# Expert outputs weighted and split at PSUM eviction, and combined by two fp32r passes with an exact one-hot matrix

## The chip, the cores and the metric

The kernel runs on one core of a Trainium2 chip, as one launch. The metric is device microseconds of one execution; the time of a kernel is the median of its runs. The engines are called by their short names below: PE (TensorE, matmuls), DVE (VectorE), ACT (ScalarE), POOL (GpSimd) and SP (SyncE, which issues the DMAs).

## What is computed

One layer of a hybrid encoder on 256 tokens of width 1024, in fp32: a mixer (attention beside a recurrence), a normalisation, and a mixture of 32 experts of which each token takes four. The change lies in the mixture, of which this is the core:

```python
logits = xt @ w_router + b_router
top_v, top_e = lax.top_k(logits, TOP_K)          # TOP_K = 4 of 32 experts
gates = jax.nn.softmax(top_v, axis=-1)
...
def expert_block(args):
    tok, g, e = args                             # the tokens of one expert
    xb = xt[tok]
    h = xb @ w_gu[e] + b_gu[e]
    y = clamped_swiglu(h) @ w_down[e] + b_down[e]
    return y * g[:, None].astype(y.dtype)        # weighted by the gate
...
out = jax.ops.segment_sum(ys.reshape(R, D), row_tok, num_segments=T)
x = layer_norm(ALPHA * x + moe(x), ln2_g, ln2_b)
```

## The kernel before

The experts' weights, 12 MB each, are streamed from HBM in transfers of 1 MB, eight of gate/up rows and four of down rows per expert, into 21 buffers that are filled in a fixed order (`load_chunk`, issued by SP). SP's and PE's instructions stand in the order of the code; those of DVE, ACT and POOL are ordered by a scheduler when the program is built. Every engine then works through its list in that order.

Each expert has 64 slots for tokens (`CAP`), and the 128 columns of PE hold two groups of 64. The loop over experts `e` does, on PE:

- `overflow(e)`: a branch on the number of the expert's tokens. Only with over 64 of them a slower spill-over pass (`more`) runs for the rest.
- `first(e)`: the gate/up matmuls `gu_mm` (L876, 64 records in the profile) into two PSUM tiles `h`, one for each half `b` of the expert's width. `swiglu` (L886 to L890) then turns each half into `g` on DVE and ACT: a minimum (L886), a sigmoid on ACT (L887), a clamp (L888), a product (L889), and the last product with the sigmoid (L890).
- `finish(e % 2)`: the combine of the pair of experts that ended before. The outputs of two experts lie in one tile of 128 partitions (64 slots each). `gt` holds, for every slot, a row over the 256 tokens with the gate at the slot's token and zero elsewhere; a matmul of `gt` with the outputs `y` (L938) adds each slot to its token, and DVE adds the result to `acc` (L940). One block of 128 tokens is done per expert: two matmuls, for the two halves of the 1024 columns.
- in an even expert `gate_rows` builds rows of gates per token for two experts on POOL; in an odd one `gate_t` transposes them into `gt` (L932, four transposes into one PSUM tile, and ACT's copy, L934).
- `act_t` for each half: two transposes of `g` (L897) and ACT's copy; `begin_gu` starts the next expert's `h` with the bias, an fp32r matmul (L668).
- `need`: the gather of the next pair's tokens (L786), and then the down matmuls `down_mm` (L909, 32 records) into the two PSUM tiles `ps[n]`.
- in an odd expert ACT copies `ps[n]` to `y` (L1105).

The PSUM tiles of `mc` (combine results, gate transposes, activation transposes, gather) share three banks. Combine and gate transposes before the change are fp32 matmuls; one fp32 matmul shows as two records of the profile, one fp32r matmul as one. Expert 31 ends differently: its weights' order, the pair before's last combines (`fin`, L1118) between the down matmuls of expert 30, and at the end ACT's and DVE's copies of `ps` (L1154, L1155), four `fin` matmuls and the last normalisation.

Of the kernel before, what the change touches and what calls it, by code (L numbers as in the profile page):

```python
# [9 lines left out]
F32 = mybir.dt.float32  # L10
F32R = mybir.dt.float32r
I32 = mybir.dt.int32
AF = mybir.ActivationFunctionType
OP = mybir.AluOpType
AX = mybir.AxisListType
ENG = mybir.EngineType

P = 128
D = 1024
T = 256  # L20
# [29 lines left out]
def trunk(ctx, tc, x, ln0_g, ln0_b, w_in, conv_w, conv_b, w_rg_a, b_rg_a, w_rg_x, b_rg_x,  # L50
# [4 lines left out]
    V, A, PE, G, SP = nc.vector, nc.scalar, nc.tensor, nc.gpsimd, nc.sync  # L55
# [14 lines left out]
    def f32(ap):  # L70
        return ap.bitcast(F32)

    def ps1(name):
        return psp.tile([P, 512], F32, tag="ps", name=name)

    def ps2(name):
        return pss.tile([P, 2, 512], F32, tag="sc", name=name)
# [129 lines left out]
    ident = keep.tile([P, P], F32, name="ident")  # L207
# [178 lines left out]
    def pj(c):  # L386
        return [psp.tile([P, 2, T], F32, tag="ps", name=f"pj{c}_{h}") for h in range(2)]
# [6 lines left out]
    ps = pj(0)  # L394
# [4 lines left out]
    ps = pj(1)  # L399
# [20 lines left out]
    ps = ps2("ps_lam")[:, 0]  # L420
# [52 lines left out]
    for b in range(4):  # L473
        V.tensor_scalar(xc[:, b], xl[:, b, 3:3 + T], pc[:, 3, b:b + 1], pc[:, 4, b:b + 1], op0=OP.mult, op1=OP.add)
        for w in range(3):
            V.scalar_tensor_tensor(xc[:, b], xl[:, b, w:w + T], pc[:, w, b:b + 1], xc[:, b],
                                   op0=OP.mult, op1=OP.add)
# [53 lines left out]
    for which, dst, bi in ((0, r_t, 5), (1, i_t, 6)):  # L531
        for h in range(2):
            ps = psp.tile([P, 2, T], F32, tag="ps", name=f"gate{which}_{h}")
            for m in range(2):
                PE.matmul(ps[:, m], wg[:, which, 2 * h + m], xc[:, 2 * h + m], start=True, stop=True)
            for m in range(2):
                b = 2 * h + m
# [29 lines left out]
    ps = ps1("gb1_ps")  # L567
# [6 lines left out]
    op = [ps2(f"op{qt}")[:, 0].rearrange("p (h c) -> p h c", h=H) for qt in range(NT)]  # L574
    for qt in range(NT):
        for h in range(H):
            for kt in range(qt + 1):
                PE.matmul(op[qt][:, h], sm[h][:, 1, (qt + kt) * P:(qt + kt + 1) * P], v_sb[:, kt, h * P:(h + 1) * P],
                          start=kt == 0, stop=kt == qt, skip_group_check=True)
# [53 lines left out]
    ps = ps2("cw_ps")[:, 0]  # L633
# [208 lines left out]
    wk = loop.enter_context(tc.tile_pool(name="wk", bufs=2, side="right", reuse_waits="tile"))  # L842
# [15 lines left out]
    def mc(name):  # L858
        return pmc[-1].tile([P, 512], F32, tag="gu", name=name)
# [52 lines left out]
    def dtiles(e):  # L912
        return [pdn.tile([P, 512], F32, tag=f"dn{n}", name=f"y{e}_{n}") for n in range(2)]

    def ytile(e, n):
        return wk.tile([P, 512], F32, tag=f"y{n}", bufs=1, name=f"ysb{e}_{n}")

    def gate_rows(e):

# [8 lines left out]
    def gate_t(e, sg):  # L928
        ps = mc(f"gt_ps{e}").rearrange("p (n t) -> p n t", n=2)
        for n in range(2):  # L930
            for t in range(NT):
                PE.transpose(ps[:, n, t * P:(t + 1) * P], sg[:, t, n * CAP:n * CAP + P], ident)  # L932
        gt = wk.tile([P, 2, T], F32, tag="gtT", bufs=1, name=f"gtT{e}")
        A.activation(gt, ps, AF.Copy)  # L934
        return gt

    def combine(t, n, y, gt, pp):
        PE.matmul(pp, gt[:, n, t * P:(t + 1) * P], y, start=True, stop=True)  # L938
        ns = slice(n * 512, (n + 1) * 512)
        V.tensor_add(acc[t][:, ns], acc[t][:, ns], pp)  # L940

# [46 lines left out]
    def ready(e):  # L988
        count(e)
        hint(f"over{e}", counts[e] > CAP)  # L990
# [24 lines left out]
    def need(i, eng, half):  # L1015
        if i < len(GROUPS):
            es = GROUPS[i]
            if i not in xgs:
                xgs[i] = gather(es, CAP, posm[:, :, es[0]:es[-1] + 1], eng, "g")
            gather_mm(*xgs[i], half)  # L1020
# [38 lines left out]
    def first(e, mid=None):  # L1059
        gi, gj = where[e]  # L1060
        ps = gu_mm(e, xgs[gi][1], gj * CAP, CAP, mid)
        ahead(e, KT)
        g = gtile(e)
        for b in range(2):
            swiglu(e, ps, b, g)
        return g

    def finish(t):

        if pend:  # L1070
            for n in range(2):
                combine(t, n, pend[0][n], pend[1], mc(f"cb{e}_{n}"))

    pend = None
    count(0)
    overflow(0)
    for e in range(NE - 1):
        if e > 0:
            overflow(e)
        ready(e + 1)  # L1080
        g = first(e, None if e else lambda i: i == 6 and need(0, V, 1))
        finish(e % 2)
        if e % 2 == 0:
            sg = gate_rows(e)
        else:
            gt = gate_t(e, sg)
        at = wk.tile([P, 4, P], F32, tag="actT", bufs=1, name=f"actT{e}")
        for b in range(2):
            act_t(e, g, b, at[:, 2 * b:2 * b + 2])
            if e < NE - 2:  # L1090
                begin_gu(e + 1, (b,))
        need(where[e][0] + 1, G, where[e][1])
        if e == LATE:
            for n in range(2):
                start_acc(n)
        if e % 2 == 0:
            ps = dtiles(e)
        if e < NE - 2:
            for j in range(4):
                down_mm(e, at, ps, j)  # L1100
            ahead(e, NH)
        if e % 2:
            pend = [ytile(e, n) for n in range(2)], gt
            for n in range(2):
                A.activation(pend[0][n], ps[n], AF.Copy)  # L1105


    smc.close()
# [5 lines left out]
    fps = [[pfin.tile([P, 512], F32, tag=f"fin{t}_{n}", name=f"fin{t}_{n}") for n in range(2)] for t in range(NT)]  # L1114

    def fin(t, a, b, ns=range(2), start=False, stop=False):
        for n in ns:
            PE.matmul(fps[t][n], a if a is ident else a[:, n, t * P:(t + 1) * P],  # L1118
                      b[n] if a is not ident else b[:, n * 512:(n + 1) * 512],
                      start=start, stop=stop, skip_group_check=True)  # L1120

    todo = [lambda t=t, n=n: fin(t, ident, acc[t], (n,), True) for t in range(NT) for n in range(2)]
    todo += [lambda n=n: fin(1, pend[1], pend[0], (n,)) for n in range(2)]
    e = NE - 1
    g = first(e, lambda i: i in FIN and todo.pop(0)())
    down_mm(e - 1, at, ps, 0)
    todo.pop(0)()
    gt = gate_t(e, sg)
    at2 = wk.tile([P, 4, P], F32, tag="xgg", bufs=3, name=f"actT{e}")
    for b in range(2):  # L1130
        act_t(e, g, b, at2[:, 2 * b:2 * b + 2])
# [8 lines left out]
    for j in range(4):  # L1140
        down_mm(e, at2, ps, j)
    of = out.rearrange("b (t p) d -> p (b t) d", p=P)
    y = [ytile(e, n) for n in range(2)]
    st2 = [wk.tile([P, 2, 6], F32, tag="st2", name=f"st2_{t}") for t in range(NT)]

    def scaled_rows(t, n):
# [4 lines left out]

    with tc.manual_schedule(engines={ENG.DVE, ENG.Activation}):
        A.activation(warm, eps_t, AF.Sqrt)
        A.activation(y[0], ps[0], AF.Copy)  # L1154
        V.tensor_copy(y[1], ps[1])  # L1155
        for t in range(NT):
            fin(t, gt, y, stop=True)
        ln2 = []
        for t in range(NT):
            for n in range(2):  # L1160
                V.bn_stats(st2[t][:, n], fps[t][n])  # L1161
                if (t, n) == (1, 0):
                    V.reciprocal(ln2[0][1], ln2[0][1])
            ln2.append(ln_var(st2[t], f"ln2_{t}", wk))
        ns = slice(512, 1024)
        mv, rs = ln2[1]
        nm = wk.tile([P, 1], F32, bufs=1, name="nm")
        a = acc[1][:, ns]
        V.scalar_tensor_tensor(acc[0][:, :512], fps[0][0], ln2[0][0][:, 0:1], lnc[0][:, :512],  # L1169
                               op0=OP.subtract, op1=OP.mult)  # L1170
        V.reciprocal(rs, rs)  # L1171
        V.tensor_scalar(nm, mv[:, 0:1], rs, -1.0, op0=OP.mult, op1=OP.mult)  # L1172
        A.activation(a, fps[1][1], AF.Identity, bias=nm, scale=rs)
        G.tensor_mul(a, a, lnc[0][:, ns])
        G.tensor_add(a, a, lnc[1][:, ns])
        V.scalar_tensor_tensor(acc[0][:, :512], acc[0][:, :512], ln2[0][1], lnc[1][:, :512], op0=OP.mult, op1=OP.add)  # L1176
        scaled_rows(0, 1)
        scaled_rows(1, 0)
# [32 lines left out]
```

## Time and profile before

| | |
|---|---|
| runs | 1108.01, 1106.1, 1108.45 us; median 1108.01 |
| profiled execution | 1107.4 us |
| its span, first to last instruction | 1105.7 us |
| PE busy | 1009.5 us, 91% of the span |
| DVE, ACT, POOL busy | 279.9, 188.7, 147.7 us |
| DMA | 423.45 MB, mean 383 GB/s |
| HBM | 420.51 MB read |
| mean granted clock of PE | 0.979 |

The profile is one execution, so it has a time of its own beside the median; its span leaves out what lies ahead of the first instruction and behind the last. The expert loop runs from about 126 us to the end. A busy share is a mean over stages; what an engine waits for in each stage is read from the trace.

### The profile page before, as it was taken

What the parts mean: (1) busy time and instruction counts of PE and PEld (TensorE: products, weight loads), DVE (VectorE), ACT (ScalarE), POOL (GpSimd) and SP (SyncE); (2) the same over time, 40 slices, a digit from 0 to 9 for tenths busy, and PEclk for the clock granted to TensorE, in tenths of its full rate; (3) what the DMA queues carried; (4) which work ended last, traced back from release to release, by engine and by line L of the source; (5) the groups of instructions that cost most, each with busy time, mean ns of one, the idle gap of its engine ahead of it and who ended that gap; (6) DMA issues with size and microseconds to landing.
All of it is one profiled execution on the core that took longest, in us unless ns stands there. A gap on an engine that the chain in (4) does not pass through costs nothing. (4 is left out here: it accounts for less than half of the span.)

```text
span 1105.7 us, 13034 instructions
## 1 busy us (share of the span) xinstructions
PE 1009.5 (91%) x4986; PEld 467.1 (42%) x4986; DVE 279.9 (25%) x623; ACT 188.7 (17%) x426; POOL 147.7 (13%) x223
## 2 busy tenths in 40 slices
PE   8999989999899999888999998889888979999996
PEld 8987633333343333334433333333323433333332
DVE  6978311121212121213112121212111122121223
ACT  5675211111111111110011111110100101111111
POOL 4583201010101010102001010101001001010101
PEclk9999999999999999999799999999999989999999
DMA  8987799999999999999999999999999999999962
GB/s 277 317 336 308 280 378 421 419 419 418 419 418 420 418 419 415 407 397 418 412 407 394 410 390 409 410 398 396 413 392 416 413 376 420 403 413 387 407 270 81
DMA packets 66135, 423.45 MB, mean 383 GB/s; under 512 B 8923, under 2 KB 8988, under 8 KB 16956
## 3 DMA queue, kind: packets, MB, share of 16 engines
q1 hardware_dynamic: 65980, 421.59, 94.5%
q8 instruction: 72, 1.18, 0.4%
q14 instruction: 83, 0.68, 0.2%
HBM read 420.51 MB, written 1.05 MB: 381 GB/s over the span
## 5 line engine op out<-in xcount | busy, mean ns | idle before, releaser
L876 PE MATMUL h<-we,xg 128*64 128x512 f32 (+1 forms) x2112 | 468.3, 601 | 69.1 <-DMA we<-in_w_gu_dram 31.2
L876 PEld LDWEIGHTS h<-we,xg 128*64 128x64 f32 (+1 forms) x2112 | 152.9, 137 | 382.2 <-issue 325.2
L909 PE MATMUL y<-we,actT 128*64 128x512 f32 x1024 | 229.9, 601 | 0.2 <-PEq L995 0.2
L886 DVE TENSOR_SCALAR g<-h 128x256 f32<-128x256 f32 x65 | 27.6, 424 | 692.8 <-PE h L876 692.8
L924 POOL TENSOR_SCALAR sgate<-iota,posm,gate 128x64 f32<-128x64 f32 x96 | 54.1, 581 | 764.3 <-PE gt_ps L932 763.3
L909 PEld LDWEIGHTS y<-we,actT 128*64 128x64 f32 x1024 | 71.5, 138 | 134.6 <-issue 129.8
L887 ACT ACTIVATE sg<-g 128x256 f32<-128x256 f32 x65 | 27.0, 416 | 593.2 <-DVE g L886 593.2
L786 PE MATMUL xg_ps<-S,n 128*128 128x128 f32 (+1 forms) x544 | 67.4, 278 | 0.0
L786 PEld LDWEIGHTS xg_ps<-S,n 128*128 128x128 f32 x544 | 66.3, 195 | 2.6 <-issue 1.6
L938 PE MATMUL cb<-ysb,gtT 128*128 128x512 f32 x116 | 57.5, 618 | 0.0
L1105 ACT ACTIVATE ysb<-y 128x512 f32<-128x512 f32 x30 | 16.3, 594 | 145.6 <-PE y L909 145.6
L940 DVE TENSOR_TENSOR acc<-acc,cb 128x512 f32<-128x512 f32 x58 | 39.4, 679 | 0.0
L794 DVE TENSOR_SCALAR xg<-xg_ps,gb 128x128 f32<-128x128 f32 (+1 forms) x68 | 22.8, 398 | 60.5 <-PE xg_ps L786 60.5
L383 PE MATMUL pj<-xo,hi 128*128 128x256 f32 x128 | 37.1, 290 | 0.7 <-DVE xo L338 0.6
L383 PE MATMUL pj<-xh,hi 128*128 128x256 f32 x128 | 37.4, 292 | 0.0
L383 PE MATMUL pj<-xh,lo 128*128 128x256 f32 x128 | 36.5, 285 | 0.0
L897 PE MATMUL actT_ps<-ident,g 128*128 128x128 f32 x130 | 29.8, 312 | 7.3 <-DVE g L890 6.3
L938 PEld LDWEIGHTS cb<-ysb,gtT 128*128 128x128 f32 x116 | 19.7, 189 | 37.5 <-ACT sg L887 22.7
L250 POOL TENSOR_TENSOR lo<-win,hi 128x1024 fp32r<-128x1024 f32 x11 | 32.8, 2999 | 13.0 <-PE pj L383 13.0
L897 PEld LDWEIGHTS actT_ps<-ident,g 128*128 128x128 f32 x130 | 21.6, 202 | 24.0 <-DVE g L890 11.5
L796 ACT ACTIVATE xg<-xg_ps,gb 128x128 f32<-128x128 f32 (+1 forms) x68 | 25.3, 451 | 31.8 <-PE xg_ps L786 31.8
L668 PE MATMUL h<-bgu,pick 128*128 128x512 f32 x64 | 30.5, 479 | 0.0
(273 smaller groups left out, 718.5 us busy)
## 6 DMA issues: line engine op xcount, KB each, us to landing
we<-in_w_gu_dram SPq DMA_DIRECT2D x256, 1024.0 KB, 20.3
we<-in_w_down_dram SPq DMA_DIRECT2D x127, 1024.0 KB, 20.8
win<-in_w_in_dram SPq DMA_DIRECT2D x8, 1024.0 KB, 11.0
wout<-in_w_out_dram SPq DMA_DIRECT2D x4, 1024.0 KB
win<-in_w_in_dram SPq DMA_DIRECT2D x4, 512.0 KB, 9.0
x<-in_x_dram SPq DMA_DIRECT2D x4, 256.0 KB, 3.4
we<-in_w_down_dram SPq DMA_DIRECT2D x2, 512.0 KB, 19.3
out_dram<-acc SPq DMA_DIRECT2D x4, 256.0 KB
```

The lines of the kernel that those rows point to most:

```text
L250: return (eng or V).tensor_sub(lo, src, f32(hi))
L383: PE.matmul(ps[m // 2][:, m % 2], a, b, start=k == 0 and m % 2 == 0 and i == 0, stop=k == KT - 1 and i == 2, skip_group_check=True)
L668: PE.matmul(ps[b], picks[e].rearrange("p g w -> p (g w)"), bgs[b], start=True, stop=False, skip_group_check=True)
L786: PE.matmul(ps[:, (k % 4) * n:(k % 4 + 1) * n], n1[t][:, k * P:(k + 1) * P], S[:, t], start=start, stop=t == NT - 1, skip_group_check=True)
L876: PE.matmul(ps[b][g * w:(g + 1) * w], xg[k // 4][:, k % 4, o:o + w], W[e, k][:, c0:c0 + 512], start=False, stop=k == KT - 1, skip_group_ch ...
L886: V.tensor_scalar(g[:, ns], ps[b][:, 0::2], 7.0, None, op0=OP.min)
L887: A.activation(s, g[:, ns], AF.Sigmoid, scale=1.702)
L897: PE.transpose(ps[:, j * P:(j + 1) * P], gj[:, j], ident)
L909: PE.matmul(ps[n][gs], at[:, 2 * b + j, g * CAP:(g + 1) * CAP], w_dn(e, 2 * g + b, j, n * 512, 512), start=c + j == 0, stop=c + j == 4, sk ...
L924: G.tensor_scalar(sg[:, t, i * CAP:(i + 1) * CAP], iota2[:, 0], posm[:, t, o:o + 1], gate[:, t, o:o + 1], op0=OP.is_equal, op1=OP.mult)
L938: PE.matmul(pp, gt[:, n, t * P:(t + 1) * P], y, start=True, stop=True)
L940: V.tensor_add(acc[t][:, ns], acc[t][:, ns], pp)
```

## The change

The gate moves from the combine's matrix into the expert outputs. `gate_t` now makes two things of the transposed gate rows, both on DVE: `gs`, the sum over the 256 tokens of each slot's row, which is the slot's gate, and `gt`, the comparison of the row with zero, an exact matrix of ones and zeros in fp32r. ACT's copy of the matrix is gone. When the outputs leave PSUM, `weighted` multiplies them by `gs` and splits them: `hi` is rounded to fp32r on ACT, `lo` is the rest, from DVE. The combine is then two fp32r matmuls, with `hi` and `lo`, in place of one fp32 matmul, and `fin` has the same two passes.

```diff
+    def weighted(e, n, src, gs):
+        hi, lo = [wk.tile([P, 512], F32R, tag=f"y{i}{n}", bufs=1, name=f"y{i}_{e}_{n}") for i in range(2)]
+        A.activation(hi, src, AF.Copy, scale=gs[:, n:n + 1])
+        V.scalar_tensor_tensor(lo, src, gs[:, n:n + 1], f32(hi), op0=OP.mult, op1=OP.subtract)
+        return hi, lo
...
-        gt = wk.tile([P, 2, T], F32, tag="gtT", bufs=1, name=f"gtT{e}")
-        A.activation(gt, ps, AF.Copy)
-        return gt
+        gs = wk.tile([P, 2], F32, tag="gs", name=f"gs{e}")
+        V.tensor_reduce(gs, ps, axis=AX.X, op=OP.add)
+        gt = wk.tile([P, 2, T], F32R, tag="gtT", bufs=1, name=f"gtT{e}")
+        V.tensor_scalar(gt, ps, 0.0, None, op0=OP.is_gt)
+        return gt, gs
 
     def combine(t, n, y, gt, pp):
-        PE.matmul(pp, gt[:, n, t * P:(t + 1) * P], y, start=True, stop=True)
+        for i in range(2):
+            PE.matmul(pp, gt[:, n, t * P:(t + 1) * P], y[i], start=i == 0, stop=i == 1)
...
-            pend = [ytile(e, n) for n in range(2)], gt
-            for n in range(2):
-                A.activation(pend[0][n], ps[n], AF.Copy)
+            pend = [weighted(e, n, ps[n], gs) for n in range(2)], gt
...
+            for i in range(2):
+                PE.matmul(fps[t][n], a[:, n, t * P:(t + 1) * P], b[n][i], start=False, stop=stop and i == 1,
+                          skip_group_check=True)
...
-        A.activation(y[0], ps[0], AF.Copy)
-        V.tensor_copy(y[1], ps[1])
+        y = [weighted(e, n, ps[n], gs) for n in range(2)]
```

The scheduler orders DVE's list anew. These are DVE's rows for odd expert 27 from the second half of the activation on (`h_1` is that half's PSUM tile, `cb_0` and `cb_1` the results of the combine, `g` the activation), before:

```order
L886 TENSOR_SCALAR g_32151<-h_1_31096 128x256
L888 TENSOR_SCALAR l_32159<-h_1_31096 128x256
L889 SCALAR_TENSOR_TENSOR l_32159<-l_32159,g_32151 128x256
L940 TENSOR_TENSOR acc_79<-acc_79,cb_0_32166 128x512
L890 TENSOR_TENSOR g_32151<-l_32159,sg_32160 128x256
L940 TENSOR_TENSOR acc_79<-acc_79,cb_1_32169 128x512
```

And the same place now, where L948 is the accumulation and L939 and L941 are the new row sum and comparison:

```order
L886 TENSOR_SCALAR g_32279<-h_1_31224 128x256
L888 TENSOR_SCALAR l_32287<-h_1_31224 128x256
L948 TENSOR_TENSOR acc_79<-acc_79,cb_0_32294 128x512
L889 SCALAR_TENSOR_TENSOR l_32287<-l_32287,g_32279 128x256
L948 TENSOR_TENSOR acc_79<-acc_79,cb_1_32298 128x512
L939 TENSOR_REDUCE gs_32307<-gt_ps_32302 128x2
L941 TENSOR_SCALAR gtT_32309<-gt_ps_32302 128x512
L890 TENSOR_TENSOR g_32279<-l_32287,sg_32288 128x256
```

Both accumulations, the row sum and the comparison now stand ahead of the last product of `g` (L890), where one accumulation stood. In an even expert (26) the rows of DVE are now these:

```order
L886 TENSOR_SCALAR g_31181<-h_1_30125 128x256
L888 TENSOR_SCALAR l_31189<-h_1_30125 128x256
L948 TENSOR_TENSOR acc_78<-acc_78,cb_0_31196 128x512
L889 SCALAR_TENSOR_TENSOR l_31189<-l_31189,g_31181 128x256
L948 TENSOR_TENSOR acc_78<-acc_78,cb_1_31200 128x512
L890 TENSOR_TENSOR g_31181<-l_31189,sg_31190 128x256
```

Before, they stood as in the odd expert; the second accumulation has moved ahead of L890 here too. On PE the list keeps its order; at the combine of expert 26 there stand four matmuls now, two into each result:

```order
L946 MATMUL cb_0_31196<-y_25_0_30165,gtT_30110 128x512
L946 MATMUL cb_0_31196<-y_25_0_30166,gtT_30110 128x512
L946 MATMUL cb_1_31200<-y_25_1_30169,gtT_30110 128x512
L946 MATMUL cb_1_31200<-y_25_1_30170,gtT_30110 128x512
```

Where one fp32 matmul with `ysb` stood for each result, a pass with `hi` and a pass with `lo` now stand one behind the other.

## Rows read from the trace of the kernel before

**Rows 1.** The page: span, PE's busy share, the granted clock and DMA in 40 slices.

```profile
span 1105.7 us, 13034 instructions
...
PE 1009.5 (91%) x4986; PEld 467.1 (42%) x4986; DVE 279.9 (25%) x623; ACT 188.7 (17%) x426; POOL 147.7 (13%) x223
...
PEclk9999999999999999999799999999999989999999
DMA  8987799999999999999999999999999999999962
```

**Rows 2.** Waits of PE, 428 to 884 us (total, times, longest).

```profile
PE h L876 <- DMA we<-in_w_gu_dram: 29.0, 36, 1.4
```

**Rows 3.** The DMA queue's waits, 428 to 884 us.

```profile
SPq L196 <- DMA we<-in_w_gu_dram: 136.1, 59, 3.1
```

**Rows 4.** Waits of PE, 885 us to the end.

```profile
PE h L876 <- DMA we<-in_w_gu_dram: 1.2, 1, 1.2
```

**Rows 5.** Timeline of PE, 928 to 985 us (start, us, what, count [idle before]).

```profile
928.85 13.95 PE L876 MATMUL h<-we,xg 128*64 128x512 f32 x64 [1.12 <-PEq L995]
942.74 1.99 PE L938 MATMUL cb<-ysb,gtT 128*128 128x512 f32 x4
944.56 0.39 PE L897 MATMUL actT_ps<-ident,g 128*128 128x128 f32 x2
...
945.05 0.50 PE L897 MATMUL actT_ps<-ident,g 128*128 128x128 f32 x2
...
955.75 13.95 PE L876 MATMUL h<-we,xg 128*64 128x512 f32 x64 [1.16 <-DMA we<-in_w_gu_dram]
969.63 1.98 PE L938 MATMUL cb<-ysb,gtT 128*128 128x512 f32 x4
...
972.54 0.50 PE L897 MATMUL actT_ps<-ident,g 128*128 128x128 f32 x2
...
983.20 2.37 PE L876 MATMUL h<-we,xg 128*64 128x512 f32 x10 [1.12 <-PEq L995]
```

**Rows 6.** Timeline of DVE, even expert 26, second half of the activation.

```profile
942.85 0.42 DVE L886 TENSOR_SCALAR g<-h 128x256 f32<-128x256 f32 x1
943.19 0.41 DVE L888 TENSOR_SCALAR l<-h 128x256 f32<-128x256 f32 x1
943.63 0.42 DVE L889 SCALAR_TENSOR_TENSOR l<-l,g 128x256 f32<-128x256 f32 x1
943.98 0.68 DVE L940 TENSOR_TENSOR acc<-acc,cb 128x512 f32<-128x512 f32 x1
944.57 0.42 DVE L890 TENSOR_TENSOR g<-l,sg 128x256 f32<-128x256 f32 x1
```

**Rows 7.** The chain that ended last, in order of time.

```profile
1091.39 0.59 ACT ysb L1154
...
1092.02 3.71 PE fin L1118 x8
...
1095.76 0.71 DVE st L1161
```

**Rows 8.** Timeline of PE, fp32r matmuls of the output projection, first and thirteenth.

```profile
108.00 0.40 PE L642 MATMUL mix<-hio,reco 128*128 128x512 f32 x1
...
110.80 0.40 PE L642 MATMUL mix<-hio,reco 128*128 128x512 f32 x1
```

**Rows 9.** Groups of DVE by shape (count | busy, mean ns | idle before).

```profile
L444 DVE TENSOR_REDUCE mx<-s 128x2 f32<-128x512 f32 x4 | 2.7, 674 | 0.0
```

**Rows 10.** Timeline of PE, last expert: a combine between down matmuls.

```profile
1080.08 1.13 PE L1118 MATMUL fin<-ysb,gtT 128*128 128x512 f32 x2
```

**Rows 11.** Timeline of the DMA queue, its last weight issues.

```profile
1044.25 20.16 SPq L196 DMA_DIRECT2D we<-in_w_down_dram  x9
```

**Rows 12.** Windows after expert 0: busy us (instructions) by engine, PEclk, DMA, GB/s.

```profile
145.20:148.50 3.30, 3.25 (x14) 3.15 (x15) 0.00 (x0) 0.69 (x2) 0.00 (x0) 0.50 1.00 420
```

**Rows 13.** Timeline of PE in expert 0, the second-half transposes.

```profile
145.25 0.70 PE L897 MATMUL actT_ps<-ident,g 128*128 128x128 f32 x2 [1.07 <-DVE g L890]
```

More of the change, by code (lines that the diff above doesn't have):

```diff
@@ L913, in dtiles @@
         return [pdn.tile([P, 512], F32, tag=f"dn{n}", name=f"y{e}_{n}") for n in range(2)]
-    def ytile(e, n):
-        return wk.tile([P, 512], F32, tag=f"y{n}", bufs=1, name=f"ysb{e}_{n}")
+    def weighted(e, n, src, gs):
[3 more added lines that the diff above has]
+        return hi, lo
     def gate_rows(e):
@@ L1085, in trunk @@
         else:
-            gt = gate_t(e, sg)
+            gt, gs = gate_t(e, sg)
         at = wk.tile([P, 4, P], F32, tag="actT", bufs=1, name=f"actT{e}")
@@ L1117, in fin @@
         for n in ns:
-            PE.matmul(fps[t][n], a if a is ident else a[:, n, t * P:(t + 1) * P],
-                      b[n] if a is not ident else b[:, n * 512:(n + 1) * 512],
-                      start=start, stop=stop, skip_group_check=True)
+            if a is ident:
+                PE.matmul(fps[t][n], a, b[:, n * 512:(n + 1) * 512], start=start, stop=stop, skip_group_check=True)
+                continue
+            for i in range(2):
+                PE.matmul(fps[t][n], a[:, n, t * P:(t + 1) * P], b[n][i], start=False, stop=stop and i == 1,
+                          skip_group_check=True)
     todo = [lambda t=t, n=n: fin(t, ident, acc[t], (n,), True) for t in range(NT) for n in range(2)]
@@ L1127, in trunk @@
     todo.pop(0)()
-    gt = gate_t(e, sg)
+    gt, gs = gate_t(e, sg)
     at2 = wk.tile([P, 4, P], F32, tag="xgg", bufs=3, name=f"actT{e}")
@@ L1142, in trunk @@
     of = out.rearrange("b (t p) d -> p (b t) d", p=P)
-    y = [ytile(e, n) for n in range(2)]
     st2 = [wk.tile([P, 2, 6], F32, tag="st2", name=f"st2_{t}") for t in range(NT)]
```

## The prediction

> **What bounds the kernel now.** I read the page first: TensorE (PE) is busy 91% of a span of 1105.7 us, and the sixteen DMA engines stand at 9 tenths in nearly every slice [rows 1]. Shares so alike do not say which of the two sets the end, so I read the waits of PE stage by stage. From 428 to 884 us PE waits 29.0 us in 36 pieces for expert weights [rows 2], and the DMA queue's waits in that stretch are for earlier weight transfers, one of three such lines alone 136.1 us [rows 3]. There the weights set the pace, and PE time saved or added is slack. Then one expert holds more than 64 tokens; its spill-over pass runs until about 900 us, and the weights get ahead. In the waits of PE from 885 us to the end [rows 4] one piece is put down to weights. It is the 1.16 us ahead of the matmul group at 955.75 [rows 5], as long as the 1.12 us at 983.20 that PE's sequencer ended (the branch ahead of each expert): not a late transfer. So from about 884 us PE's own sequence sets the end: experts 25 to 31. **Only there does the change count.** A change of PE's cadence ahead of 884 us is absorbed as long as a pair of experts stays under the weights' pace.
>
> Next I read that sequence, for an even and an odd expert [rows 5]. After the gate/up matmuls PE runs the combine (from 942.74 or 969.63), for odd experts the gate transposes, then the transposes of the first half of the activation (944.56 in the even one), those of the second half (945.05, 972.54), and the gather. The second half needs VectorE (DVE) to have finished `g` for it. DVE gets that half of `h` at 942.85, and its last multiply runs from 944.57 to 944.99 [rows 6]; PE starts 0.06 later. So the combine is not plain cost: it is the work that covers the activation's latency.
>
> **The change, part by part.**
>
> *Combine on PE.* Before: four matmul records from 942.74 to the next start at 944.56 [rows 5], 1.82 us. After: four fp32r matmuls. Twelve steps between fp32r matmuls of that shape, from 108.00 to 110.80, give 0.233 us each [rows 8]. The old records step by 0.44 (the last eight in 3.71, the last of them lasting some 0.62 [rows 7]), so of the 1.82 up to 0.1 is the first one's start; with it the four take 1.03 us: 0.8 us saved an expert. The upper bound for a pass is the old 0.44.
>
> *DVE's queue.* The order of rows shown with the change is what decides. In an even expert both accumulations of the combine now stand ahead of the last multiply of `g`, where one stood. In an odd expert the row sum and the comparison of the gate matrix stand there too, and they wait for transposes that come behind the combine on PE. Steps between starts come from [rows 6]: 0.34 from 942.85 to 943.19, 0.35 from 943.63 to 943.98, and 0.59 from an accumulation to what follows it (943.98 to 944.57).
>
> Even: 943.19 + 0.34 (accumulation) + 0.59 (next step) + 0.35 (accumulation) + 0.59 = 945.06 for the multiply, 945.48 for its end, and PE at 945.54 instead of 945.05: **0.49 us later**, although the combine ended 0.8 us earlier. The first accumulation is ready in time: two passes from 942.74 end about 943.5.
>
> Odd: DVE gets `h` 0.11 us behind the combine's start again (942.74 and 942.85 in the even one), so at 969.74, and the same steps put the second accumulation at 971.36 and the row sum at 971.95. Its transposes are done by then: they are no longer than the 0.49 us of the first-half pair and its bias, and the combine now ends at 970.66. A row sum over 512 elements takes 674 ns [rows 9], near the accumulation's 0.68, and the comparison is such a pass over PSUM as well, so I give both a step of 0.60: the multiply at 973.15, its end at 973.57, PE at 973.63 instead of 972.54: **1.09 us later**. Everything behind follows on PE at once (bias, gather, down), and the PSUM buffers that they wait for are read out before that, so nothing later takes the delay back. Per expert the bounds are nothing, if PE were covered otherwise, and 0.6 and 1.4 with every added DVE step at its full 0.68.
>
> The step of 0.59 after an instruction that lasts 0.68 [rows 6] shows successive DVE instructions overlapping by about 0.09 us. The Trainium skill says otherwise in VectorE: DVE Perf Modes, "The DRAIN you can't avoid": the next operation does not start until the pipe has emptied. By that, one added step in an even and three in an odd expert would cost 0.09 more each, 1.1 us more over the six experts; the rows of this trace do not agree with it.
>
> *Splitting the outputs.* ScalarE's two passes stay two; DVE gains two passes per pair of experts, behind the down matmuls. PE needs the pieces only at the next combine, a gate/up block of 13.95 us later [rows 5]: no cost. Without that cover it would be 0.6 to 0.7 us a piece, as at the end [rows 7].
>
> *Gate matrix.* One ScalarE pass less per pair; ScalarE's next work there is not what PE waits for. No gain.
>
> *The last expert.* The combine of the pair before stands twice between down matmuls (the first at 1080.08, two records in 1.13 us [rows 10]). After: two passes save 2 x (0.44 - 0.233) = 0.41 each, and what a switch of tile shape costs stays; **0.8 us**. Its DVE work has ended by then, so nothing is uncovered.
>
> *The final combine.* Now one 0.59 us pass precedes the matmuls (1091.39, with eight records in 3.71 from 1092.02) and DVE's last statistics start at 1095.76 [rows 7]. After: ScalarE's two passes at 1091.39 and 1091.88, DVE's pieces 0.66 us apart from about 1092.04, the last matmul done about 1094.8; but DVE's four statistics can start only behind its second piece, about 1093.36, and with the small operations between them (four times 0.6 us and less) the last starts about 1095.5. **0.2 us saved**, bounds nothing and 1.0.
>
> *Sum.* From 884 us on there are three odd (25, 27, 29) and three even (26, 28, 30) experts with a combine: 3 x 1.09 + 3 x 0.49 = 4.7; less 0.8, less 0.2: **+3.7 us**. A pair now takes from 928.85 to 983.20 us [rows 5], 54.4 us, and would take 56.0, still under the 59.5 us that 24 transfers of 2.48 us take (nine issues, eight steps, each when an earlier transfer lands, lie within 20.16 us, the last one lasting 0.33 [rows 11]), so the stretch ahead of 884 us hides its share. The profiled execution took 1107.4 us, 1.7 above its span and 0.6 under the median of 1108.0. 1107.4 + 3.7 = 1111.1, which I take; from the median it would be 1111.7.
>
> **Rivals.**
>
> *PE's saving counts (faster).* If `g` were ready by the time PE gets to it, six combines give 6 x 0.8 = 4.8, and the end 1.0: 1101.6 us. It decides from the point where DVE's multiply ends before PE gets to the second-half transposes, which the shorter combine puts at about 944.3; by the rows above it ends at 945.48. For it speaks that PE shows no idle time ahead of those transposes before the change [rows 5]; against it the order shown with the change, which DVE keeps. Chance 0.12.
>
> *Hidden either way (no change).* If weights paced the last 200 us too, the loss would lie in their slack: 1107.2 to 1108. The waits of the end [rows 4] speak against it; a loss smaller than worked out, 2 us or less, ends here as well. Chance 0.16.
>
> *fp32r passes no faster in this place.* At 0.44 a pass, the combine lasts as before, the first accumulation starts at 943.98 instead of 943.53, and the multiply is late by another 0.45: 3 x (1.54 + 0.94) = 7.4, no saving at the end: 1114.8. The steps of 0.233 [rows 8] speak against it. Chance 0.05.
>
> *The clock falls (slower still).* PE would idle 1.5 us (even) to 2 us (odd) ahead of the second-half transposes. In the first expert, which has no combine, PE idled 1.07 us ahead of these transposes, and from there the granted clock was 0.50 for 3.3 us [rows 12, 13], that is 1.2 instead of 2.4 GHz; a stretch like it costs about 1.6 us of PE work. Once in each odd expert of the last stretch would make 1107.4 + 3.7 + 4.8 = 1115.9; once in each of the six, 1121. Against it: behind the 36 waits of [rows 2], up to 1.4 us long and in close sequence, the clock line of [rows 1] stays at 9 but for two slices. Chance 0.12. TensorE: Matmul & The Clock Gate (the Trainium skill, Part 1) says that the clock falls when the engine idles and Part 4 that transposes do not count as activity; by that the gap would be longer than its idle time, and this rival likelier. The trace agrees so far as these rows go.
>
> **How the numbers follow.** My forecast has 0.55. A measurement of this kernel tells about 0.2%, 2.2 us. Forecast: 1109 to 1113, from the bounds 0.6 and 1.4 at the top and a step of DVE hidden at the bottom. With the no-change case below and the clock above, the range is 1106.5 to 1115.5, which leaves out the faster rival and the worst of the clock. Slower: 0.55 + 0.05 + 0.12, less 0.04 of the forecast that stays under 2.2 us, 0.68; same 0.16 + 0.04 = 0.20; faster 0.12.
>
> **What would show it.** Right: in experts 25 to 30 PE's combine takes about 1.0 us; PE idles before the second-half transposes, released by DVE's `g` multiply, 1.5 us in even and 2 us in odd experts; the pair's period is 1.6 us longer from 928 us on, and unchanged (weight-paced) before 884 us; PE's waits for weights in the middle shrink by what the waits for `g` grow. Wrong: no such wait; a DVE order other than the one shown; a granted clock of 0.50 inside the loop; or weights late after 900 us.

## The result and the profile after

The changed kernel takes 1115.59 us (median of four runs, 1115.04 to 1117.19) against 1107.54 in the same series (1106.1 to 1108.45): 1.0069 times the kernel before, 95% interval 1.0049 to 1.0089. The profiled execution took 1115.48 us, 8.1 more than that of before. Slower, as forecast, but by more than twice the 3.7 us of the forecast, at the upper end of the range (1115.5).

The page of the changed kernel, span, busy shares, granted clock and DMA as in [rows 1]:

```profile
span 1113.6 us, 13093 instructions
...
PE 996.6 (89%) x4986; PEld 479.0 (43%) x4986; DVE 318.3 (29%) x686; ACT 184.3 (17%) x411; POOL 151.0 (14%) x223
...
PEclk9999999999999999998799999999999889999998
DMA  8897799999999999999999999999999989999932
```

PE has 12.9 us less to do, and the span is 7.9 us longer. The mean granted clock fell from 0.979 to 0.961. In a slice of 28 us a low stretch of 3.4 us hardly shows in tenths, so the clock line alone would have hidden it.

The waits of PE, first from 428 to 884 us (total, times, longest), to be held against [rows 2]:

```profile
PE actT_ps L897 <- DVE g L890: 21.7, 15, 1.8
PE h L876 <- DMA we<-in_w_gu_dram: 6.9, 7, 1.5
```

and from 885 us to the end, against [rows 4]:

```profile
PE actT_ps L897 <- DVE g L890: 12.3, 7, 3.2
...
PE h L876 <- DMA we<-in_w_gu_dram: 1.2, 1, 1.2
```

Ahead of 884 us the new wait for `g` (21.7) stands in place of the old wait for weights (29.0, now 6.9): PE arrives later and finds its weights there (22.1 us less of the one wait, 21.7 more of the other). Behind 885 us nothing is there to be replaced, and the wait for `g` is plain loss. (The 3.2 of it is the spill-over pass's, which before had too.)

PE's timeline in odd expert 27 and even expert 28 (start, duration, what [idle before]), against [rows 5]:

```profile
975.16 0.50 PE L897 MATMUL actT_ps<-ident,g 128*128 128x128 f32 x2
...
977.72 0.48 PE L897 MATMUL actT_ps<-ident,g 128*128 128x128 f32 x2 [1.83 <-DVE g L890]
...
978.27 2.77 PE L786 MATMUL xg_ps<-S,n 128*128 128x128 f32 x16
...
1003.92 1.20 PE L946 MATMUL cb<-y,gtT 128*128 128x512 f32 x4
1004.96 0.39 PE L897 MATMUL actT_ps<-ident,g 128*128 128x128 f32 x2
...
1006.71 0.50 PE L897 MATMUL actT_ps<-ident,g 128*128 128x128 f32 x2 [1.12 <-DVE g L890]
```

and in odd expert 29:

```profile
1035.30 0.48 PE L897 MATMUL actT_ps<-ident,g 128*128 128x128 f32 x2 [1.83 <-DVE g L890]
...
1035.84 1.95 PE L786 MATMUL xg_ps<-S,n 128*128 128x128 f32 x16
```

The combine takes 1.04 us (1003.92 to 1004.96) where it took 1.82, and the second-half transposes wait: 1.12 us in the even expert, 1.83 in the odd one. What DVE did meanwhile in expert 27, against [rows 6]:

```profile
974.42 0.68 DVE L948 TENSOR_TENSOR acc<-acc,cb 128x512 f32<-128x512 f32 x1
975.02 0.42 DVE L889 SCALAR_TENSOR_TENSOR l<-l,g 128x256 f32<-128x256 f32 x1
975.36 0.68 DVE L948 TENSOR_TENSOR acc<-acc,cb 128x512 f32<-128x512 f32 x1
975.95 0.68 DVE L939 TENSOR_REDUCE gs<-gt_ps 128x2 f32<-128x512 f32 x1
976.55 0.68 DVE L941 TENSOR_SCALAR gtT<-gt_ps 128x512 fp32r<-128x512 f32 x1
977.15 0.42 DVE L890 TENSOR_TENSOR g<-l,sg 128x256 f32<-128x256 f32 x1
```

These are the steps of the prediction: 0.60, 0.34, 0.59, 0.60, 0.60, and PE starts behind the end of L890.

The rest shows in the windows of experts 28, 29 and 27, of a piece of expert 27 and of one of expert 25 (busy us of each engine with its instructions, then granted clock, DMA share, GB/s):

```profile
990.04:1017.33 27.29, 25.08 (x122) 10.39 (x123) 5.17 (x12) 3.41 (x10) 0.00 (x0) 1.00 1.01 418
1017.33:1045.93 28.60, 25.64 (x126) 10.81 (x127) 7.14 (x17) 2.70 (x6) 3.59 (x6) 1.00 1.01 420
959.76:990.04 30.28, 27.26 (x127) 11.68 (x127) 7.20 (x17) 2.96 (x7) 5.26 (x10) 0.94 1.01 421
979.20:982.61 3.41, 3.41 (x14) 2.07 (x14) 1.37 (x4) 0.00 (x0) 1.40 (x4) 0.50 1.01 420
...
921.18:924.60 3.42, 3.42 (x16) 2.84 (x17) 0.54 (x2) 0.14 (x1) 0.79 (x2) 0.50 1.03 431
```

Experts 27 and 29 do the same work with the same 1.83 us wait, and one takes 1.68 us more. From 979.20, 1.5 us behind the end of its wait, PE's granted clock is 0.50 for 3.41 us, 1.2 instead of 2.4 GHz: the gather of 978.27, which runs into it, takes 2.77 us, and 1.95 in expert 29. Expert 25 has such a stretch from 921.18, expert 29 has none. Ahead of 884 us there are others behind the waits of odd experts, the first at 228.27; there the weights set the pace.

The stages below carry all experiments. Each column is the distance of two starts of gate/up matmuls on PE, from the expert's start to that of the next, and the last one from expert 30's start to the end of the span, in us, each from the one profiled execution of its kernel:

| kernel | 25 | 26 | 27 | 28 | 29 | 30 to end |
|---|---|---|---|---|---|---|
| before | 28.89 | 26.90 | 27.45 | 26.83 | 27.45 | 68.18 |
| changed | 31.90 | 27.30 | 30.28 | 27.29 | 28.60 | 67.67 |
| changed, again | 31.66 | 27.30 | 30.19 | 27.29 | 28.60 | 67.68 |
| gate_behind | 28.92 | 27.37 | 27.46 | 27.29 | 27.38 | 67.67 |
| order_of_before | 30.47 | 26.95 | 27.50 | 26.89 | 27.50 | 67.25 |
| filler | 31.19 | 27.29 | 28.66 | 27.29 | 28.64 | 67.66 |
| before_late | 31.65 | 26.83 | 31.71 | 26.82 | 31.46 | 68.19 |
| gather_first | 28.27 | 26.92 | 26.81 | 26.93 | 26.88 | 67.67 |
| gather_split | 28.18 | 26.93 | 26.80 | 26.91 | 26.81 | 67.66 |
| gather_split_order | 28.58 | 26.92 | 27.09 | 26.91 | 26.98 | 67.25 |
| evict_behind | 29.39 | 25.91 | 26.97 | 25.92 | 27.09 | 67.26 |
| evict_behind_before | 28.61 | 26.70 | 27.15 | 26.68 | 27.22 | 68.17 |

Row "changed" against row "before": +3.01, +0.40, +2.83, +0.46, +1.15, -0.51, and +0.60 ahead of expert 25, together the 7.9 us of the span.

### The profile page after: what moved, and what is told of

The parts are those of the page before. It is cut to its first block, busy times and chain, and to the rows that moved or that the text cites. A ratio compares the mean times of both kernels' runs of the same rounds, so it can differ in the third digit from the quotient of the medians.

```text
span 1113.6 us, 13093 instructions
## 1 busy us (share of the span) xinstructions
PE 996.6 (89%) x4986; PEld 479.0 (43%) x4986; DVE 318.3 (29%) x686; ACT 184.3 (17%) x411; POOL 151.0 (14%) x223
## 3 DMA queue, kind: packets, MB, share of 16 engines
HBM read 420.51 MB, written 1.05 MB: 379 GB/s over the span
## 5 line engine op out<-in xcount | busy, mean ns | idle before, releaser
L876 PE MATMUL h<-we,xg 128*64 128x512 f32 (+1 forms) x2112 | 462.1, 601 | 46.3 <-PEq L1003 17.8
L928 POOL TENSOR_SCALAR sgate<-iota,posm,gate 128x64 f32<-128x64 f32 x96 | 57.1, 612 | 745.6 <-PE gt_ps L936 744.6
L786 PEld LDWEIGHTS xg_ps<-S,n 128*128 128x128 f32 x544 | 77.7, 222 | 3.0 <-issue 1.6
L786 PE MATMUL xg_ps<-S,n 128*128 128x128 f32 (+1 forms) x544 | 78.8, 308 | 0.0
L919 DVE SCALAR_TENSOR_TENSOR y<-y,gs,y 128x512 fp32r<-128x512 f32 x32 | 22.6, 747 | 106.5 <-ACT y L918 106.5
L918 ACT ACTIVATE y<-y,gs 128x512 fp32r<-128x512 f32 x32 | 20.2, 684 | 176.7 <-PE y L909 168.2
L948 DVE TENSOR_TENSOR acc<-acc,cb 128x512 f32<-128x512 f32 x58 | 39.4, 680 | 0.0
L898 ACT ACTIVATE actT<-actT_ps 128x256 f32<-128x256 f32 x64 | 24.5, 383 | 80.6 <-PE actT_ps L897 80.6
L250 POOL TENSOR_TENSOR lo<-win,hi 128x1024 fp32r<-128x1024 f32 x11 | 33.0, 3018 | 13.0 <-PE pj L383 12.9
L946 PE MATMUL cb<-y,gtT 128*128 128x512 f32 x116 | 34.8, 421 | 0.0
```

Source lines behind the costliest of these rows:

```text
L250: return (eng or V).tensor_sub(lo, src, f32(hi))
L786: PE.matmul(ps[:, (k % 4) * n:(k % 4 + 1) * n], n1[t][:, k * P:(k + 1) * P], S[:, t], start=start, stop=t == NT - 1, skip_group_check=True)
L876: PE.matmul(ps[b][g * w:(g + 1) * w], xg[k // 4][:, k % 4, o:o + w], W[e, k][:, c0:c0 + 512], start=False, stop=k == KT - 1, skip_group_ch ...
L928: G.tensor_scalar(sg[:, t, i * CAP:(i + 1) * CAP], iota2[:, 0], posm[:, t, o:o + 1], gate[:, t, o:o + 1], op0=OP.is_equal, op1=OP.mult)
L946: PE.matmul(pp, gt[:, n, t * P:(t + 1) * P], y[i], start=i == 0, stop=i == 1)
```

## The experiments

Theory A: DVE's new order opens the waits (the forecast's +3.7 us), and the long waits of odd experts bring the low clock (the rest). Theory B: the clock falls for another reason, the fp32r matmuls or the idle time in sum. Theory C: the rest is late weights. Each ratio below is to the kernel before, with its 95% interval; it is made from the single runs of a series and need not equal the quotient of the two medians.

**The changed kernel again**, beside later experiments on another chip. 

> The changed kernel itself, beside the experiments on the same chip. If what was measured first holds: 1114 to 1117 us, 1.005 to 1.009 of the kernel before, with a granted clock of 0.50 for 3.4 us behind some odd experts after 900 us.

1115.78 us (median of 6), 1.0078 of the kernel before (1.0055 to 1.0102). The low stretches stand in the same experts, 25 and 27, for 3.41 us from 927.23 and from 985.25, and again none in 29. (Its profiled execution was the slowest of the six, 1122.78 us; the table's stages of 25 to 30 are those of the first profile within 0.24 us.)

**Only the gate matrix behind the product** (`gate_behind`; `last` holds the two final instructions of `swiglu`):

```diff
-            gt, gs = gate_t(e, sg)
+            with tc.issue_after(last[1].ins):
+                gt, gs = gate_t(e, sg)
```

> The changed kernel, with the row sum and the comparison of the gate matrix queued on VectorE behind the last product of g in odd experts (both accumulations stay ahead of it). Theory A (VectorE's order opens the gaps, and the long gap of the odd experts brings the low clock): in odd experts the 1.83 us wait of PE falls into two of about 0.8 us each, one ahead of the second-half transposes and one ahead of the gather, which now waits for the PSUM buffer that the comparison frees; odd experts 0.6 us longer than before, even ones 0.45, less 1.0 at the end: 1109.6 us, and no stretch at a granted clock of 0.50 behind experts 26 to 29. Theory B (the clock falls because of the fp32r matmuls or of the idle time in sum, however it is cut): the low stretches stay, 1113 to 1114. Theory C (what the forecast missed is late weights): about 1115, with waits for weights behind 900 us.

1109.13 us against 1107.44 (ratio 1.0005, 0.9985 to 1.0025), 6.5 under the changed kernel, and no low stretch between 904 and 1098 us. Odd expert 27 on PE:

```profile
973.51 0.48 PE L897 MATMUL actT_ps<-ident,g 128*128 128x128 f32 x2 [0.63 <-DVE g L890]
...
974.05 1.95 PE L786 MATMUL xg_ps<-S,n 128*128 128x128 f32 x16
```

The odd expert's wait fell from 1.83 to 0.63 and its length to that of before. The expected second wait, of the gather for the comparison's PSUM bank, did not come: the gather starts at 974.05, and DVE's comparison runs from 973.88. The even experts keep their +0.46. So the two gate operations, and not the accumulations, made the odd experts late. The idle time in sum fell as well (PE is busy 135.2 of the 145 us from 905 to 1050 us, and 131.6 in the changed kernel), so this run alone does not tell the length of one wait from the sum.

**DVE's order of before, all else changed** (`order_of_before`, in addition to the edit above):

```diff
             for n in range(2):
-                combine(t, n, pend[0][n], pend[1], mc(f"cb{e}_{n}"))
+                with tc.issue_after(last[n].ins):
+                    combine(t, n, pend[0][n], pend[1], mc(f"cb{e}_{n}"))
```

> The changed kernel with VectorE's order of the kernel before: the first accumulation behind the product with l, the second behind the last product of g, and the gate matrix's two operations behind that. Theory A: even experts as before (the multiply ends 2.2 us behind the combine's start, where PE got to it at 2.3), odd ones 0.6 longer, since the gather waits for the comparison's PSUM buffer; less 1.0 at the end: 1108.3 us, 1107.5 to 1109.5, no low clock behind experts 26 to 29. Theory B: low stretches stay, 1111 to 1113. Theory C (weights): about 1115.

1108.51 us (ratio 0.9998, 0.9977 to 1.0019). Its profiled execution, 1114.91 us, is 6.4 us late at expert 0 already (132.7 us against 126.3), most of it a wait of PE for DVE in the mixer (5.09 us, ended at 70.74) that the profile of before does not have, so only the stages are compared: experts 26 to 29 are 0.05 us longer than before, even and odd alike, and the end 0.93 shorter. With the order restored the 0.8 us that each combine saves on PE returns as waits, in even expert 26 as 0.73 us for `g`, and in odd expert 27 as these:

```profile
979.63 0.51 PE L897 MATMUL actT_ps<-ident,g 128*128 128x128 f32 x2 [0.34 <-DVE acc L948]
...
980.61 0.51 PE L897 MATMUL actT_ps<-ident,g 128*128 128x128 f32 x2 [0.24 <-ACT actT L898]
```

The activation's latency sets the expert's length; a shorter combine alone buys nothing.

**The wait filled with work** (`filler`): four (even) or seven (odd) more bias matmuls in fp32r between the two halves of the transposes, into a PSUM tile that the true one starts anew. Nothing else is moved.

```diff
             ps[b] = pgu[-1].tile([P, 512], F32, tag="gu", name=f"h{e}_{b}")
+            for i in range(fill if b == 0 else 0):
+                PE.matmul(ps[b], picks[e].rearrange("p g w -> p (g w)"), bgs[b], start=True, stop=True,
+                          skip_group_check=True)
```

> The changed kernel with extra work for PE alone: between the two halves of the activation's transposes it runs four (even experts) or seven (odd) bias matmuls of 128x512 in fp32r more, 0.23 us each, into the next expert's PSUM tile, which the true bias matmul then starts anew. The wait for g stays as long, PE is busy through most of it. Theory A: VectorE's lateness stays (odd 1.1 us, even 0.45 over before), the low stretches behind experts 25 to 28 go: 1107.4 + 3.8 = 1111.2 us, 1110.5 to 1112.5. If the clock has no part in it: 1115 to 1116.

1112.18 us (ratio 1.0035, 1.0014 to 1.0056), 3.4 under the changed kernel although PE does more. PE in odd expert 27, and the windows of 27 and 29:

```profile
974.19 1.86 PE L669 MATMUL h<-bgu,pick 128*128 128x512 f32 x7
...
976.51 0.48 PE L900 MATMUL actT_ps<-ident,g 128*128 128x128 f32 x2 [0.23 <-DVE g L893]
```

```profile
958.53:987.19 28.66, 27.25 (x133) 12.06 (x134) 7.20 (x17) 2.94 (x7) 5.29 (x10) 1.00 1.01 420
...
1014.48:1043.12 28.64, 27.25 (x133) 12.04 (x134) 7.18 (x17) 2.74 (x6) 3.61 (x6) 1.00 1.01 414
```

The lateness is all there (28.66, as expert 29 of the changed kernel with 28.60), the clock stays at 1.00, and expert 27 no longer differs from 29. Nor is that one lucky profile: its twelve runs have mean granted clocks of 0.972 to 0.981, the ten of the changed kernel 0.955 to 0.967. This separates the two costs: the lateness of `g`, and the clock, which falls when PE idles and not when the same time passes in matmuls.

**A long wait without the change** (`before_late`): the kernel before with three DVE passes over the gate matrix, of which nobody reads the result, ahead of the last product (`last.pop()()`) in odd experts. They are work added to the reference's.

```diff
+            for i in range(3):
+                dd = wk.tile([P, 2, T], F32, tag="dead", bufs=1, name=f"dead{e}_{i}")
+                x = V.tensor_scalar(dd, ps, 0.0, None, op0=OP.is_gt)
+            with tc.issue_after(x.ins):
+                last.pop()()
```

> The kernel before, with its exact plain passes and its undivided outputs, and with three passes of VectorE over the gate matrix whose result nobody reads, put ahead of the last product of g in odd experts (both accumulations then stand ahead of it too). Each pass has the comparison's form, a step of 0.6 us; the gate transposes end 2.3 us behind the combine's start, so the multiply ends at about 4.5 and PE waits 1.6 to 2.0 us ahead of the second-half transposes of odd experts, about as long as in the changed kernel (1.83); even experts are as before. Theory A (a long gap of PE is enough to bring the low clock): 3 x 1.7 = +5.1 from the gaps and 1.7 for each low stretch, of which two or three show behind experts 25 to 29: 1115 to 1118. Theory B (the low clock needs the fp32r combine as well): 1112 to 1113 and no low stretch there.

1122.77 us (ratio 1.0158, 1.0134 to 1.0183): more than expected, since the wait became 2.73 us (the passes also waited 0.38 us for ACT's copy of the same tile and took 0.71 each). Expert 27 on PE, and windows behind the waits of experts 25, 27 and 29:

```profile
980.17 0.70 PE L897 MATMUL actT_ps<-ident,g 128*128 128x128 f32 x2 [2.73 <-DVE g L890]
```

```profile
923.20:926.60 3.40, 3.40 (x25) 2.67 (x27) 0.93 (x3) 0.58 (x2) 1.10 (x3) 1.00 1.02 424
980.19:983.60 3.41, 3.41 (x15) 3.31 (x16) 0.00 (x0) 0.69 (x2) 0.38 (x1) 0.50 1.02 423
1038.22:1041.63 3.41, 2.93 (x13) 2.83 (x14) 0.43 (x2) 0.39 (x1) 0.88 (x2) 0.50 1.02 423
```

The plain fp32 combine is in place and the clock falls: the wait is enough without fp32r, and theory B falls in that half. Its other half, idle time in sum, is not excluded by `gate_behind` and `filler`, which cut the sum together with the single wait. Where the stretches begin, beside the long waits of odd experts and never beside the 1.1 us of even ones (counted in the last section), speaks against a sum over many experts; one long wait and several waits close together were not told apart. And not every long wait does it: expert 25 kept 1.00 and paid 2.76 us, the wait alone, while 27 and 29 paid 4.26 and 4.01.

**A longer piece of work over the wait** (`gather_first`): the gather of the next pair's half moves ahead of the activation's transposes, DVE's evictions of it stay behind the last product; DVE's order is otherwise the changed kernel's.

```diff
+        with tc.issue_after(last[1].ins):
+            need(where[e][0] + 1, G, where[e][1])
         at = wk.tile([P, 4, P], F32, tag="actT", bufs=1, name=f"actT{e}")
         for b in range(2):
             act_t(e, g, b, at[:, 2 * b:2 * b + 2])
...
-        need(where[e][0] + 1, G, where[e][1])
```

> The changed kernel with the gather of the next pair's half moved ahead of the activation's transposes on PE, where it covers the wait for g (its own evictions on VectorE stay behind the last product of g). Theory A: the gather's 1.95 us is longer than the wait, so PE shows no idle time ahead of the transposes in experts 25 to 29, the 0.8 us that the combine saves counts in each, expert 30 (no gather) keeps its gap: 5 x (-0.8) + 0.45 - 1.0 = -4.5, 1102.9 us, 1101.5 to 1105 with the weights as the floor, no low clock behind experts 26 to 29. Theory B or C: no better than 1108.

1106.19 us (ratio 0.9979, 0.9956 to 1.0002). The wait for `g` is gone in experts 25 to 29, no low stretch stands between 903 and 1096 us, and odd experts are 0.6 us shorter than before. Even ones gain nothing, since the wait has moved:

```profile
944.56 0.39 PE L897 MATMUL actT_ps<-ident,g 128*128 128x128 f32 x2
...
946.12 2.37 PE L909 MATMUL y<-we,actT 128*64 128x512 f32 x10 [0.94 <-ACT actT L898]
```

**The gather's evictions behind.** Two attempts to leave ACT's evictions of the gather behind its copies of the activation by writing them later in the code:

```diff
         for k in ks:
             for t in range(NT):
                 gather_ps(S, ps, k, t, t == 0)
+        if later is not None:
+            later.append(lambda: [gather_out(S, xg[half], ps, k) for k in ks])
+            return
```

The list `later` is called behind `act_t`.

> The changed kernel with the gather's matmuls ahead of the activation's transposes, and the gather's evictions on ScalarE and VectorE left behind the copies of the transposed activation, where they stood. In the run before this one the even experts lost what the moved gather gave, 0.94 us, to a wait of the down matmuls for ScalarE's copy, which stood behind four gather evictions. If that was the cause, even experts 26 and 28 now gain as the odd ones did (0.6 us each over the kernel before): 1.2 to 1.9 us less than with the evictions moved, some 1103 us in the profile and 1104.5 in the median. If the down matmuls wait for something else, no change from 1106.

> The same, and VectorE in the order of the kernel before. Expert 30, which has no gather to cover its wait, then waits 0.37 us less (0.98 instead of 1.35); in the others the gather covers the wait in either order: 0.4 us less than with the changed kernel's order, which the times can hardly tell from nothing.

1107.19 (ratio 1.0003, 0.9987 to 1.0019) and 1106.25 us (0.9990, 0.9978 to 1.0001). The even experts stay as they were, because the scheduler put the evictions first again, as ACT's timeline in expert 28 of the first of the two shows:

```profile
1004.65 1.50 ACT L796 ACTIVATE xg<-xg_ps,gb 128x128 f32<-128x128 f32 x4 [1.97 <-PE xg_ps L786]
1006.03 0.67 ACT L901 ACTIVATE actT<-actT_ps 128x256 f32<-128x256 f32 x2
```

These two did not test the idea. The second, in DVE's order of before, shows the 0.4 us of expert 30 (67.25 against 67.66 to 67.67). Then the order was forced (`evict_behind`, with DVE's order of before):

```diff
-            act_t(e, g, b, at[:, 2 * b:2 * b + 2])
+            copied = act_t(e, g, b, at[:, 2 * b:2 * b + 2])
...
+        with tc.issue_after(copied.ins):
+            for f in later:
+                f()
```

> As the last (gather's matmuls ahead of the transposes, VectorE in the order of the kernel before), with the gather's evictions on ScalarE held behind the copies of the transposed activation. In the run before, the scheduler had put the four evictions ahead of these copies in even experts again, and the down matmuls still waited 0.94 us for ScalarE there. If those four evictions are the cause, that wait goes in experts 26 and 28, odd ones stay: 2 x 0.94 = 1.9 us less, 1104.4 us, 0.997 of the kernel before. If the wait has another cause, no change from 1106.3.

1105.08 us (ratio 0.9976, 0.9964 to 0.9987): faster than both kernels. PE and ACT in even expert 28:

```profile
997.59 1.95 PE L786 MATMUL xg_ps<-S,n 128*128 128x128 f32 x16
999.37 0.40 PE L900 MATMUL actT_ps<-ident,g 128*128 128x128 f32 x2
...
1000.40 1.94 PE L912 MATMUL y<-we,actT 128*64 128x512 f32 x8
```

```profile
999.80 0.85 ACT L901 ACTIVATE actT<-actT_ps 128x256 f32<-128x256 f32 x2 [2.21 <-PE actT_ps L900]
1000.55 1.50 ACT L796 ACTIVATE xg<-xg_ps,gb 128x128 f32<-128x128 f32 x4
```

PE runs from combine to gather, transposes and down matmuls without a wait, and even experts take 25.9 us, 1.0 less than before. In odd ones the gather waits 0.34 us for an accumulation. From 905 to 1050 us PE's waits name no weights and no `g`:

```profile
PE h L879 <- PEq L1006: 4.4, 4, 1.1
PE h L879 <- issue: 1.6, 2, 1.2
PE xg_ps L786 <- DVE acc L951: 1.0, 3, 0.3
```

**The same move made to the kernel before** (`evict_behind_before`). 

> A control: the same move of the gather's matmuls and evictions, made to the kernel before, where the plain combine covers the wait for g already. If what the last kernel gains over the kernel before comes from the shorter combine and only the cover was missing: nothing here, 1107.0 to 1108. If the move of the gather pays by itself: 1104 to 1105.

1106.24 us (ratio 0.9987, 0.9974 to 0.9999): a gain of about 0.1%, where nothing was expected. Its experts 26 to 29 take 107.75 us together, those of before 108.63, those of `evict_behind` 105.89. So in this stretch a third of the gain is the move's own (0.9 of 2.7 us), and two thirds, with the 0.9 at the end, need the shorter combine. The move's 0.9 lies between the combine's start and the first down matmul: 4.77 us in even and 5.36 in odd experts of before, 4.63 and 5.07 here. In odd ones 0.18 of it is that the second-half transposes start 0.65 us behind the first-half ones in before and 0.47 here; no profile shows PE idle there, and what released it was not found. The medians stand only 1.2 us apart; `evict_behind` starts expert 25 2.2 us later in its profiled execution, and what makes the stretch ahead of it vary was not tested.

## Why the forecast was right in direction and short in size

- *Weights set the pace ahead of 884 us, PE behind it.* Right. The wait for `g` took the place of the wait for weights, and all but 0.60 us of the loss starts with expert 25. Late weights (theory C) are excluded by the waits behind 885 us, 1.2 us before and after.
- *Combine, 0.8 us saved.* Right: 1.04 us for four passes, 1.03 forecast. `order_of_before` shows that the saving is worth nothing by itself. The rival by which it counts fell, until the gather covered the latency.
- *Even experts 0.49 us later.* Measured +0.40 and +0.46, and 0.42 in expert 30 (67.67 against 67.25 with DVE's order of before). The idle time of 1.5 us that the prediction named for even experts does not follow from its own rows, by which PE gets to the second-half transposes at 944.3 and starts them at 945.54, 1.2 us; the trace has 1.12, and 1.83 where it named 2 for odd ones.
- *Odd experts 1.09 us later.* Expert 29 of the changed kernel, at full clock, +1.15; 27 and 29 of `filler`, +1.21 and +1.19. `gate_behind` shows that the row sum and the comparison carry it. The two rules for DVE's steps can be told apart here: the rows gave 1.09, and the pipe that empties between operations (the Trainium skill, VectorE: DVE Perf Modes, "The DRAIN you can't avoid") would have made it 1.36. The trace has steps of 0.59 to 0.60 between starts of 0.68 us operations; the measurement decides for the rows. The prediction quoted only half of that section: it goes on that a next operation that is not held starts earlier, and these steps agree with that half.
- *The end, -1.0.* Right: with DVE's order of before the last column is 0.93 shorter. The combines between the down matmuls take 0.73 us each (1089.02 and 1091.55) where [rows 10] had 1.13, and from ACT's first eviction (1099.52) to DVE's last statistics (1103.72) it is 4.20 us, against 4.37 in [rows 7].
- *The sum.* 3 x 1.15 + 0.40 + 0.46 + 0.42 - 0.93 = +3.8, where 3.7 was forecast. `filler`, in which these terms alone are left, measured +4.7; its profiled execution has a low stretch of 6.8 us around the start of expert 25, where before has 3.4.
- *The clock.* This is the term that was mis-sized: it stood beside the sum as a rival with a chance of 0.12, and at nothing in it. Measured, it took 1.68 us in expert 27 and 3.01 - 1.15 = 1.86 in expert 25, of which 0.26 stands in that expert's gate/up matmuls (15.58 us against 15.32; both kernels have a low stretch about their start, from 900.70 in the changed one and from 899.48 before) and 1.6 in the new stretch: the price that the prediction had put on one. That makes 3.5 of the 7.9 us. The +0.60 ahead of expert 25 was not taken apart; in it the spill-over pass has 13.65 us at 0.50 from 880.22, where before has 3.41 and 6.83. The rival's own time, with one low stretch in each of three odd experts, was 1115.9, nearer to the 1115.59 measured than the 1111.1 taken, although only two of the three came; and "a granted clock of 0.50 inside the loop" was among the prediction's signs of being wrong.

The argument against the clock was that the 36 waits of [rows 2], at most 1.4 us, left the clock line at 9. That reading fails in the very trace that it was taken from. PE waited 1.42 us for weights until 728.53, and from 728.81 its granted clock was 0.50 for 3.41 us, in a slice that shows 9; four shorter waits for weights, 0.17 to 0.64 us, stand in the 10 us ahead of it:

```profile
728.90:732.20 3.30, 3.30 (x10) 1.20 (x8) 1.60 (x4) 0.42 (x1) 0.00 (x0) 0.50 0.93 367
```

The precedent that the prediction had, expert 0, did fall with 1.07 us ahead of the same transposes [rows 12, 13], though PE had idled 1.06 us ahead of the first-half ones as well, ended at 143.45. TensorE: Matmul & The Clock Gate (the Trainium skill, Part 1 and Part 4) spoke for the fall: the clock drops when the engine idles, and transposes do not count as activity. The trace agrees as far as `filler` goes, where matmuls in the gap, among the same transposes, kept 1.00; that the transposes themselves do not count was not tested.

Expectations of experiments that failed: that the gather would wait for the comparison's PSUM bank (`gate_behind`, and the 0.6 us that it was to cost odd experts in `order_of_before`); the length of the wait in `before_late`; the gain of the even experts in `gather_first` (1101.5 to 1105 us expected, 1106.19 measured) and again in `gather_split`, which ACT's evictions took; and that the move would bring the kernel before nothing. Open are why a wait brings the low clock in one odd expert and not in the next (25 and 27 but not 29; in `before_late` 27 and 29 but not 25), what makes up the +0.60 ahead of expert 25, and what the second-half transposes of odd experts wait for in before.

## What to carry to other kernels

Work that stands between a producer and its consumer on a busy engine may be cover, not cost: ask what the next instruction waits for before counting a shorter stage as a gain, and look in the new order of the side engine for what now stands ahead of that product. If a forecast opens idle time on TensorE, put the clock's price into the sum with a probability per wait (here ten of fifteen for 1.8 us) instead of leaving it a rival, and look for low stretches in windows of a few us: the clock line of the page hides them. A shorter stage pays once other ready work is moved into the gap and its own evictions are queued behind what the critical engine waits for.

## What was not expected of the hardware

The same wait, in the same place of the same program, brought the low clock or not: 2.73 us in `before_late` left expert 25 at 1.00 and put experts 27 and 29 at 0.50 for 3.41 us each, at a cost of 1.3 to 1.5 us beyond the wait. Counted over the whole loop of the changed kernel, where PE waited for `g` in 15 odd experts for 1.8 us or more, a stretch at 0.50 began within 1.5 us of the end of the wait in ten (one of them just ahead of a spill-over pass, which has low stretches in every kernel); in its second profile in ten of 15; in `before_late`, with 2.7 us, within 0.6 us in eleven of 15. Behind the 14 waits of 1.1 to 1.2 us in even experts none began, in either profile of the changed kernel or in `gate_behind`. Yet shorter ones in a row could do it: in expert 0 of the kernel before 1.06 and 1.07 us, ended 1.80 us apart [rows 12, 13], and in the changed kernel 1.05 and 1.01 us there did not.
